# Rounded and remainder products of successive weight tiles in alternating order

## The chip, the core and the metric

One NeuronCore of a Trainium2 chip runs the kernel in one launch. TensorE (PE in the profile) multiplies, VectorE (DVE) and ScalarE (ACT) work on tiles in SBUF and PSUM, and SyncE (SP) issues the DMA transfers from HBM. The metric is the device time of one execution in microseconds (us), as the median of several runs; lower is better.

## The reference, cut

What is computed is one encoder block on 256 tokens of width 2048, all in fp32: a gated feed-forward network (half weight), a token mixing stage of 16 attention heads, and a second feed-forward network. Nine vectors that come from `silu(c) @ w_ada` shift, scale and gate the stages.

```python
def swiglu(x, w_gate, w_up, w_down):
    return (jax.nn.silu(x @ w_gate) * (x @ w_up)) @ w_down

mod = jax.nn.silu(c) @ w_ada[l] + b_ada[l]
sh1, sc1, gt1, sh2, sc2, gt2, sh3, sc3, gt3 = jnp.split(mod, N_MOD, axis=-1)
f = swiglu(modulate(rms_norm(h, g_ffn1[l]), sh1, sc1), w1_gate[l], w1_up[l], w1_down[l])
h = h + 0.5 * gt1[:, None, :] * f
...
qkv = modulate(rms_norm(h, g_mix[l]), sh2, sc2) @ w_qkv[l]
...
mix = jnp.concatenate([o_na, o_dil], axis=-1) @ w_o[l]
h = h + gt2[:, None, :] * mix
f = swiglu(modulate(rms_norm(h, g_ffn2[l]), sh3, sc3), w2_gate[l], w2_up[l], w2_down[l])
h = h + 0.5 * gt3[:, None, :] * f
```

D_MODEL is 2048, D_FF 5632, SEQ 256.

## The kernel before

**Products.** An fp32 product is made of three faster ones in the rounded type fp32r. Every weight tile of 128x1024 (eight blocks of 128x128) is brought from HBM into a buffer `raw` (tile `rw`, five buffers), rounded by ACT into `hi` (`hiw`, line 144, four buffers), and DVE writes the remainder `raw - hi` into `lo` (`low`, line 147, four buffers). The activations stand the same way in two halves side by side: `r[:, 0, :]` is rounded, `r[:, 1, :]` the remainder, 256 columns each (`nx` for the inputs of the up and gate products, `hd` for the inputs of the down products). One matmul with a block of `hi` streams both halves, 512 columns; one with a block of `lo` streams the rounded half alone, 256 columns, and adds to the first half of the same PSUM bank.

**Order on PE.** `W.add` (line 320) collects eight blocks, that is one weight tile. Then it issues the eight products with `hi` (line 338) and after them the eight with `lo` (line 340). So PE runs eight matmuls of 512 columns, eight of 256, eight of 512, and so on. A sum (one PSUM bank, or one half of a pair of banks) may begin and end inside a tile: its first `hi` product carries `start`, which clears the bank, and its last `lo` product carries `stop`. `then` is the code that reads a finished sum, such as `up_finish`, `up_fold` or the update of `h` in `ffn_down`.

**Stages.** Tiles that pass through `W.add` are numbered here from 0, in the order in which they are used, over all weight matrices:

| stage | tiles | time in the trace, us | blocks of a sum |
|---|---|---|---|
| 1a: first 6 of 16 input blocks of the up and gate products (`up_first`, tile `pa`) | 0 to 35 | 65 to 173 | 6 |
| 1b: the other 10 (`pb`) | 36 to 115 | 173 to 397 | 10 (first four pairs 6 and 4) |
| 1d: down products over 32 of 44 hidden blocks (`pd`) | 116 to 179 | 397 to 576 | 32 |
| 1c: the last 12 hidden blocks (`pb`) | 180 to 227 | 576 to 710 | 16 |
| 1e: their down products (`pd`) | 228 to 251 | 710 to 778 | 12 |
| attention: q, k, v and output projection, own order of products | 252 to 379 | 782 to 1189 | |
| 2a, 2b, 2d, 2c, 2e: the second network in the same way, no part of 6 | 380 to 643 | 1198 to 1937 | 16, 16, 32, 16, 12 |

In 1a four sums of six blocks fill three tiles: in the first tile of three both sums begin, in the second the first four blocks belong to a sum that is already open, in the third the first two do.

**What sets the order.** A scheduler orders the instructions of each engine by its own estimate of when operands are ready; inside `manual_schedule` regions the named engines follow the order of the code. Each engine then runs its queue strictly in that order. `W.prepare` (line 303) makes the cast and the remainder of a tile three tiles ahead of its use. A cast has to wait until the products with the `hi` of four tiles earlier are done, a remainder for the products with that `lo`. In the same DVE queue stand the products of `w_ada` (line 127, tiles `ra` and `rx`, 128x2048 each, paced by `ws.pace`), and in the same ACT queue the copies of finished sums in 1a (line 356, `pt<-pa`).

Of the kernel before, what the change touches and what calls it, by code (L numbers as in the profile page):

```python
# [15 lines left out]
P = 128  # L16
S = 256
D = 2048
KT = D // P
# [45 lines left out]
def build(tc, a):  # L65
    nc = tc.nc
    with ExitStack() as ctx:
# [42 lines left out]
        nx = [cp.tile([P, 2, S], F32R, tag=f"nx{k}", name=f"nx{k}") for k in range(KT)]  # L110
# [167 lines left out]
        first = {}  # L278
# [5 lines left out]
        class W:  # L284
            def __init__(self):
                self.head = 0
                self.tail = 0
                self.todo = []
                self.thens = []
                self.ready = {}  # L290
                self.rate = 0.0
                self.credit = 0.0

            def fetch(self, n):
                while self.head < n:
                    self.ready[self.head] = wraw(srcs[self.head])
                    self.head += 1
# [19 lines left out]
                self.tail += 1  # L317
                return self.ready.pop(self.tail - 1)

            def add(self, out, r, first, last, then=None, whole=False):  # L320

                self.todo.append((out, r, first, last, whole))
                if then:
                    self.thens.append(then)
                if len(self.todo) < 8:
                    return
                hi, lo = self.chunk()
                todo, thens = self.todo, self.thens  # L330
                self.todo, self.thens = [], []
                for b, (out, r, first, last, whole) in enumerate(todo):
                    w = hi[:, b * P : (b + 1) * P]
                    if whole:
                        nc.tensor.matmul(out[:, :S], w, r[:, 0, :], start=first, stop=False)
                        nc.tensor.matmul(out[:, :S], w, r[:, 1, :], start=False, stop=False)
                    else:
                        nc.tensor.matmul(out, w, r, start=first, stop=False)  # L338
                for b, (out, r, first, last, whole) in enumerate(todo):
                    nc.tensor.matmul(out[:, :S], lo[:, b * P : (b + 1) * P], r[:, 0, :], start=False, stop=last)  # L340
                for then in thens:
                    then()

# [4 lines left out]
        ws = W()  # L348
# [14 lines left out]
        def up_mm(ps, k0, k1, first, last, then=None):  # L363
            for j in range(2):
                for k in range(k0, k1):
                    end = k == k1 - 1
                    ws.add(ps[:, j, :], nx[k], first and k == k0, last and end, then if end and j else None)

        def up_finish(f, ps, part, hid):
            if f in part:  # L370
# [14 lines left out]
        def ffn_down(fs, hid, gate, stat=None, out=None, order=None):  # L385
            acc_ = {}
            for d, f in down_order(fs):
                if d not in acc_:
                    acc_[d] = bank("pd")
                if stat is not None and d == KT // 2 and f == fs[0]:  # L390
                    bg_until(0)
                if order is not None and d == KT - 4 and f == fs[0]:
                    order.enter_context(tc.manual_schedule(engines=STARTUP))
                whole = d == KT - 1 and fs[-1] == FT - 1
                end = f == fs[-1]

                def update(d=d, whole=whole):
                    ps = acc_[d]
                    if stat is not None:
                        stat.fold()  # L400
                    for part_ in (ps[:, :S], ps[:, S:])[: 1 if whole else 2]:
                        nc.vector.scalar_tensor_tensor(h[d], part_, gate(d), h[d], ALU.mult, ALU.add)  # L402
                    if stat is not None:
                        stat.add(h[d], late=d >= KT - 4)
                    if out is not None:
                        nc.sync.dma_start(out[d], h[d])

                ws.add(acc_[d], hid[f], f == fs[0], end, update if end else None, whole)

        def ffn(kx, part, ready_k, gate, stat=None, out=None, order=None):  # L410

# [64 lines left out]
        with tc.manual_schedule(engines=STARTUP):  # L476
# [53 lines left out]
        with tc.tile_pool(name="att", bufs=2) as ap_, tc.tile_pool(name="atc", bufs=1) as ac:  # L530
# [201 lines left out]
            last = [j * KT + k for k in range(K2, KT) for j in (7, 6)]  # L732
# [41 lines left out]
            last = [8 * KT + k for k in range(KT)]  # L774
# [10 lines left out]
        hid = {}  # L785
        ps2 = [pair("pb") for f in range(NG)]
        for k in range(KT):
            if k % 2 == 0 and k + 2 < KT:
                norm_pair((k + 2, k + 3), r3, 6, 7)
            for f in range(NG):  # L790
                for j in range(2):
                    ws.add(ps2[f][:, j, :], nx[k], k == 0, k == KT - 1)
        order.close()
        for f in range(NG):
            up_finish(f, ps2[f], {}, hid)
# [1 line left out]
        for f in range(NG, F1):  # L797
            ps = pair("pb")
# [108 lines left out]
```

## Time and profile before

| | us |
|---|---|
| median of 3 runs | 1945.46 |
| the runs | 1944.61, 1949.75, 1945.46 |
| the profiled execution | 1942.14 |
| its span, first to last instruction | 1940.4 |
| PE busy, share of the span | 1899.4, 98% |
| DVE busy | 1523.3, 79% |
| ACT busy | 907.5, 47% |

The profile is one execution. 1.74 us of its 1942.14 lie outside the span. PE is busy nearly all the time, but matmuls overlap in the records (the 512-column ones last about 0.39 us each and start about 0.23 us apart), so what a matmul costs is read from the distance of starts, not from its duration.

### The profile page before, as it was taken

The numbers are of one execution on the slowest core, as the hardware profiler recorded it, in microseconds if no ns is written. First come the engines' busy times: TensorE is split into PE (matmuls) and PEld (weight loads), VectorE is DVE, ScalarE is ACT, GpSimd is POOL, SyncE is SP. The second block draws the span as 40 slices with busy tenths as digits, with TensorE's granted clock in tenths as the row PEclk, the third lists the DMA queues.
The fourth block names the chain that finished last, engine by engine and source line by source line (L and its number), as shares of the span: only waits on it lengthen the run. The fifth ranks groups of instructions, "written<-read, shape, count | busy, mean of one in ns | idle before, by whom it ended". The sixth has DMA issues, their size and how long they took to land.

```text
span 1940.4 us, 27380 instructions
## 1 busy us (share of the span) xinstructions
PE 1899.4 (98%) x10504; PEld 1648.6 (85%) x10504; DVE 1523.3 (79%) x2055; ACT 907.5 (47%) x1332; POOL 0.7 (0%) x6
## 2 busy tenths in 40 slices
PE   7999999999999999899999998999999999999999
PEld 6878888888888888688888887888888888888888
DVE  7898999999878889699986898668865555555665
ACT  2444544443334454445555565544444433334442
POOL 0000000000000000000000000000000000000000
PEclk9999999999999999999999999999999999999999
DMA  9998888899989898598865544668865666666664
GB/s 392 386 340 303 315 305 309 305 329 395 356 302 345 310 321 311 171 326 324 318 222 165 163 142 146 192 213 318 323 206 186 188 190 186 190 189 187 191 194 134
DMA packets 120083, 503.98 MB, mean 260 GB/s; under 512 B 13328, under 2 KB 15632, under 8 KB 101520
## 3 DMA queue, kind: packets, MB, share of 16 engines
q1 hardware_dynamic: 119952, 502.24, 74.5%
q8 instruction: 82, 1.34, 0.3%
q14 instruction: 49, 0.40, 0.1%
HBM read 500.09 MB, written 2.10 MB: 259 GB/s over the span
## 4 chain that ended last, share of the span: by engine, by line
PE 53%; DVE 4%; issue 1%; ACT 1%; DMA 0%; SPq 0%; ACTq 0%; DVEq 0%
PE pb L338 17%; PE pb L340 9%; PE pd L338 8%; PE pd L340 4%; PE pqq L606 3%; PE pqk L606 3%; PE pqv L606 3%; DVE low L147 2%; PE pqq L609 1%; PE pqk L609 1%; PE pqv L609 1%; PE pso L643 1%; DVE wt L633 1%; PE psc L153 0%; PE po L153 0%
## 5 line engine op out<-in xcount | busy, mean ns | idle before, releaser
L144 ACT CAST hiw<-rw 128x1024 fp32r<-128x1024 f32 x644 | 675.0, 1051 | 793.8 <-PE pd L338 233.7
L147 DVE TENSOR_TENSOR low<-rw,hiw 128x1024 fp32r<-128x1024 f32 x644 | 783.4, 1221 | 293.9 <-ACT hiw L144 286.8
L338 PE MATMUL pb<-nx,hiw 128*128 128x512 f32 x2432 | 610.5, 393 | 4.1 <-DVE nx L221 4.1
L338 PEld LDWEIGHTS pb<-nx,hiw 128*128 128x128 f32 x2432 | 438.4, 189 | 83.0 <-issue 4.4
L340 PEld LDWEIGHTS pb<-nx,low 128*128 128x128 f32 x2432 | 331.7, 190 | 24.5 <-DVE low L147 0.8
L338 PE MATMUL pd<-hd,hiw 128*128 128x512 f32 x1384 | 346.7, 392 | 0.0
L340 PE MATMUL pb<-nx,low 128*128 128x256 f32 x2432 | 339.2, 282 | 0.4 <-DVE low L147 0.4
L338 PEld LDWEIGHTS pd<-hd,hiw 128*128 128x128 f32 x1384 | 248.9, 189 | 44.4
L127 DVE CUSTOM_DVE_ANT_0 ra<-ra,cb,vec 128x2048 f32<-128x2048 f32 x109 | 255.7, 2346 | 11.4 <-DMA ra<-in_w_ada_dram 11.3
L340 PEld LDWEIGHTS pd<-hd,low 128*128 128x128 f32 x1408 | 191.7, 190 | 13.6 <-DVE low L147 0.3
L340 PE MATMUL pd<-hd,low 128*128 128x256 f32 x1408 | 196.5, 282 | 0.0
L402 DVE SCALAR_TENSOR_TENSOR h<-pd,m,h 128x256 f32<-128x256 f32 x126 | 59.5, 481 | 59.4 <-PE pd L340 59.0
L127 DVE CUSTOM_DVE_ANT_0 rx<-rx,cb,vec 128x2048 f32<-128x2048 f32 x35 | 82.1, 2346 | 2.1 <-DMA rx<-in_w_ada_dram 2.1
L338 PE MATMUL pa<-nx,hiw 128*128 128x512 f32 x288 | 72.6, 394 | 6.2 <-ACT hiw L144 6.2
L606 PE MATMUL pqv<-hiw,nx 128*128 128x512 f32 x256 | 66.7, 403 | 5.4 <-ACT nx L219 5.4
L338 PEld LDWEIGHTS pa<-nx,hiw 128*128 128x128 f32 x288 | 51.7, 189 | 16.7 <-ACT hiw L144 7.4
L606 PE MATMUL pqk<-hiw,nx 128*128 128x512 f32 x256 | 65.4, 396 | 0.3 <-ACT hiw L144 0.3
L606 PE MATMUL pqq<-hiw,nx 128*128 128x512 f32 x256 | 64.6, 394 | 0.0
L643 PE MATMUL pso<-ox,hiw 128*128 128x512 f32 x248 | 64.2, 402 | 0.0
L606 PEld LDWEIGHTS pqv<-hiw,nx 128*128 128x128 f32 x256 | 48.3, 193 | 17.8 <-ACT nx L219 7.9
L606 PEld LDWEIGHTS pqk<-hiw,nx 128*128 128x128 f32 x256 | 46.4, 188 | 9.5 <-ACT hiw L144 0.7
L606 PEld LDWEIGHTS pqq<-hiw,nx 128*128 128x128 f32 x256 | 46.8, 188 | 9.1
(143 smaller groups left out, 1370.9 us busy)
## 6 DMA issues: line engine op xcount, KB each, us to landing
ra<-in_w_ada_dram SPq DMA_DIRECT2D x109, 1024.0 KB, 7.3
rw<-in_w_b_dram SPq DMA_DIRECT2D x200, 512.0 KB, 4.4
rw<-in_w_d_dram SPq DMA_DIRECT2D x128, 512.0 KB, 4.3
rw<-in_w_c_dram SPq DMA_DIRECT2D x96, 512.0 KB, 3.6
rw<-in_w_qkv_dram SPq DMA_DIRECT2D x96, 512.0 KB, 4.4
rx<-in_w_ada_dram SPq DMA_DIRECT2D x35, 1024.0 KB, 7.1
rw<-in_w_e_dram SPq DMA_DIRECT2D x48, 512.0 KB, 4.6
rw<-in_w_a_dram SPq DMA_DIRECT2D x44, 512.0 KB, 5.3
```

The source lines that it names most:

```text
L127: dot = nc.vector.tensor_tensor_reduce(out=raw, in0=raw, in1=cb, scale=1.0, scalar=vec[:, BA + i : BA + i + 1], op0=ALU.mult, op1=ALU.add, ...
L144: cast = nc.scalar.copy(hi, raw)
L147: nc.vector.tensor_tensor(lo, raw, hi.bitcast(F32), ALU.subtract)
L338: nc.tensor.matmul(out, w, r, start=first, stop=False)
L340: nc.tensor.matmul(out[:, :S], lo[:, b * P : (b + 1) * P], r[:, 0, :], start=False, stop=last)
L402: nc.vector.scalar_tensor_tensor(h[d], part_, gate(d), h[d], ALU.mult, ALU.add)
L606: nc.tensor.matmul(ps[t], nx[k][:, i, t * P : (t + 1) * P], whi[:, kk * 512 : (kk + 1) * 512], start=k + i == 0, stop=False)
L609: nc.tensor.matmul(ps[t], nx[k][:, 0, t * P : (t + 1) * P], wlo[:, kk * 512 : (kk + 1) * 512], start=False, stop=k == KT - 1)
L633: nc.vector.scalar_tensor_tensor(t, t if u < END else ps[:, :S], gt2[:, d : d + 1], rows[b], ALU.mult, ALU.mult)
L643: nc.tensor.matmul(ps, w, o, start=kk == 0, stop=False)
```

## The change

A tile now begins with remainder products where the tile before ended with them. `ended_lo` remembers this. Each block carries a `key`, the sum to which it belongs. Blocks whose sum begins in this tile can't go first with `lo`, since the `hi` product has to clear the bank over all 512 columns; they are `late`, the others are `early` if the tile before ended with `lo`. Order in a tile: `lo` of the early blocks, `hi` of all eight, `lo` of the late ones. `stop` goes to whichever product of a block comes last. A tile in which all blocks are early ends with `hi`, and the next tile begins with `hi` again.

```diff
-                self.todo.append((out, r, first, last, whole))
+                self.todo.append((out, r, first, last, whole, key))
...
+                new = {t[5] for t in todo if t[2]}
+                early = [b for b in range(8) if todo[b][5] not in new] if self.ended_lo else []
+                late = [b for b in range(8) if b not in early]
+
+                def low(b, stop):
+                    out, r = todo[b][:2]
+                    nc.tensor.matmul(out[:, :S], lo[:, b * P : (b + 1) * P], r[:, 0, :], start=False, stop=stop)
+
+                for b in early:
+                    low(b, False)
+                for b, (out, r, first, last, whole, key) in enumerate(todo):
                     w = hi[:, b * P : (b + 1) * P]
+                    stop = last and b in early
                     if whole:
                         nc.tensor.matmul(out[:, :S], w, r[:, 0, :], start=first, stop=False)
-                        nc.tensor.matmul(out[:, :S], w, r[:, 1, :], start=False, stop=False)
+                        nc.tensor.matmul(out[:, :S], w, r[:, 1, :], start=False, stop=stop)
                     else:
-                        nc.tensor.matmul(out, w, r, start=first, stop=False)
-                for b, (out, r, first, last, whole) in enumerate(todo):
-                    nc.tensor.matmul(out[:, :S], lo[:, b * P : (b + 1) * P], r[:, 0, :], start=False, stop=last)
+                        nc.tensor.matmul(out, w, r, start=first, stop=stop)
+                for b in late:
+                    low(b, todo[b][3])
+                self.ended_lo = bool(late)
```

The keys are `(id(ps), j)` in `up_mm`, `d` in `ffn_down` and `(f, j)` in stage 2a. No instruction is added or removed on any engine. The attention part, which doesn't use `W.add`, keeps its order on all engines; on DVE, ACT and SP the scheduler moves instructions of the feed-forward stages by up to five places.

How often PE goes from a `lo` to a `hi` product, counted in the built programs:

| stage | 1a | 1b | 1d | 1c | 1e | 2a | 2b | 2d | 2c | 2e |
|---|---|---|---|---|---|---|---|---|---|---|
| before | 35 | 80 | 64 | 48 | 24 | 7 | 120 | 64 | 48 | 24 |
| after | 47 | 66 | 33 | 24 | 16 | 4 | 60 | 33 | 24 | 16 |

PE in stage 1d, where tile 130 ends and tile 131 begins (`low_3858` is the remainder of tile 130, `hiw_3888` and `low_3889` are the halves of 131); before:

```order
L340 MATMUL pd_3885<-hd21_2905,low_3858 128x256
L340 MATMUL pd_3885<-hd22_2985,low_3858 128x256
L340 MATMUL pd_3885<-hd23_3038,low_3858 128x256
L338 MATMUL pd_3885<-hd24_3118,hiw_3888 128x512
L338 MATMUL pd_3885<-hd25_3175,hiw_3888 128x512
L338 MATMUL pd_3885<-hd26_3256,hiw_3888 128x512
```

and now:

```order
L340 MATMUL pd_3885<-hd21_2905,low_3858 128x256
L340 MATMUL pd_3885<-hd22_2985,low_3858 128x256
L340 MATMUL pd_3885<-hd23_3038,low_3858 128x256
L340 MATMUL pd_3885<-hd24_3118,low_3889 128x256
L340 MATMUL pd_3885<-hd25_3175,low_3889 128x256
L340 MATMUL pd_3885<-hd26_3256,low_3889 128x256
```

The eight remainder products of tile 131 have moved ahead of its eight rounded ones, so PE asks for `low_3889` when the tile begins and not eight matmuls later.

PE in stage 1a, where tile 4 ends and tile 5 begins (`low_469` belongs to tile 4, `hiw_500` and `low_501` to tile 5, a third tile of three); before:

```order
L340 MATMUL pa_550<-nx1_100,low_469 128x256
L340 MATMUL pa_550<-nx2_101,low_469 128x256
L340 MATMUL pa_550<-nx3_102,low_469 128x256
L338 MATMUL pa_550<-nx4_103,hiw_500 128x512
L338 MATMUL pa_550<-nx5_104,hiw_500 128x512
```

and now:

```order
L340 MATMUL pa_550<-nx2_101,low_469 128x256
L340 MATMUL pa_550<-nx3_102,low_469 128x256
L340 MATMUL pa_550<-nx4_103,low_501 128x256
L340 MATMUL pa_550<-nx5_104,low_501 128x256
L351 MATMUL pa_550<-nx4_103,hiw_500 128x512
```

Two remainder products of tile 5 now stand ahead of its rounded ones. In the second tile of three the scheduler also sends one to four `hi` products of the new sum ahead of the four early `lo` ones.

ACT at the same place (`pt10_573` is the copy of the sum that ends in tile 4); before:

```order
L144 CAST hiw_468<-rw_466 128x1024
L144 CAST hiw_500<-rw_498 128x1024
L356 COPY pt10_573<-pa_523 128x512
L230 ACTIVATE nx7_106<-nt_583,m0_78 128x256
L144 CAST hiw_526<-rw_524 128x1024
```

and now:

```order
L144 CAST hiw_468<-rw_466 128x1024
L370 COPY pt10_573<-pa_523 128x512
L144 CAST hiw_500<-rw_498 128x1024
L230 ACTIVATE nx7_106<-nt_583,m0_78 128x256
L144 CAST hiw_526<-rw_524 128x1024
```

The copy and the cast of tile 5 have changed places. Before, the copy of a sum that ends in tile n-1 stood directly ahead of the cast of tile n at tiles 11, 17, 26 and 32; now it does so at 5, 11, 17, 26 and 32, all of them third tiles of three.

## Rows read from the trace of the kernel before

**Rows 1.** The page's part 1, busy time of PE, PE's weight loads, DVE, ACT and POOL:

```profile
PE 1899.4 (98%) x10504; PEld 1648.6 (85%) x10504; DVE 1523.3 (79%) x2055; ACT 907.5 (47%) x1332; POOL 0.7 (0%) x6
```

**Rows 2.** Windows of 50 and 100 us in stages 1a, 1b and 2b: start:end, length, then busy us (and instructions) of PE, PEld, DVE, ACT and POOL, the granted PE clock as a share of 2.4 GHz, DMA share, GB/s:

```profile
100.00:150.00 50.00, 47.30 (x269) 40.99 (x268) 47.37 (x54) 24.29 (x32) 0.00 (x0) 1.00 0.92 342
300.00:350.00 50.00, 50.00 (x289) 44.00 (x288) 48.89 (x67) 23.98 (x33) 0.00 (x0) 1.00 0.85 292
...
1600.00:1700.00 100.00, 100.00 (x576) 88.02 (x575) 50.67 (x55) 37.76 (x36) 0.00 (x0) 1.00 0.61 188
```

**Rows 3.** Timeline of PE around one tile of stage 1d, read through slits so narrow that single matmuls show (first number: start, us): the first and the sixth `hi` product of the tile, its first `lo` product, and the first `hi` product of the next tile:

```profile
503.25 0.40 PE L338 MATMUL pd<-hd,hiw 128*128 128x512 f32 x1
...
504.41 0.39 PE L338 MATMUL pd<-hd,hiw 128*128 128x512 f32 x1
...
505.09 0.40 PE L340 MATMUL pd<-hd,low 128*128 128x256 f32 x2
...
506.04 0.40 PE L338 MATMUL pd<-hd,hiw 128*128 128x512 f32 x1
```

**Rows 4.** Timeline of PE at four places: `hi` runs of tiles 396 and 499 in stage 2b (103 tiles apart); eight 512-column products of the q, k, v projection that follow other 512-column ones, and what follows them; and the end of the kernel, where the last weight tiles run as 256-column products throughout:

```profile
1246.97 2.00 PE L338 MATMUL pb<-nx,hiw 128*128 128x512 f32 x8
...
1534.69 2.00 PE L338 MATMUL pb<-nx,hiw 128*128 128x512 f32 x8
...
871.34 1.98 PE L606 MATMUL pqv<-hiw,nx 128*128 128x512 f32 x8
873.15 1.07 PE L609 MATMUL pqv<-low,nx 128*128 128x512 f32 x4
...
1934.17 0.28 PE L335 MATMUL pd<-hd,hiw 128*128 128x256 f32 x1
...
1936.09 1.12 PE L340 MATMUL pd<-hd,low 128*128 128x256 f32 x8
```

**Rows 5.** Who waited for whom in stage 1a, 60 to 185 us (us in total, times, longest), and, as the last line, the same view of the whole span for the casts and the `hi` products of stages 1b, 1c, 2b and 2c:

```profile
ACT pt L356 <- PE pa L340: 55.4, 24, 4.2
...
PE pa L338 <- ACT hiw L144: 6.2, 5, 1.6
...
PE pa L340 <- DVE low L147: 0.6, 2, 0.4
PE pb L340 <- DVE low L147: 0.4, 1, 0.4
...
ACT hiw L144 <- PE pb L338: 171.8, 117, 2.0
```

**Rows 6.** Timeline at tile 17 of stage 1a, on PE (the `lo` run of tile 16, the `hi` run of tile 17), ACT (copy, cast) and DVE (remainder of tile 17):

```profile
114.60 1.11 PE L340 MATMUL pa<-nx,low 128*128 128x256 f32 x8
116.85 2.11 PE L338 MATMUL pa<-nx,hiw 128*128 128x512 f32 x8 [1.15 <-ACT hiw L144]
...
115.27 0.58 ACT L356 COPY pt<-pa 128x512 f32<-128x512 f32 x1 [4.25 <-PE pa L340]
115.75 1.05 ACT L144 CAST hiw<-rw 128x1024 fp32r<-128x1024 f32 x1
...
116.83 1.23 DVE L147 TENSOR_TENSOR low<-rw,hiw 128x1024 fp32r<-128x1024 f32 x1 [0.26 <-ACT hiw L144]
```

**Rows 7.** The same at tile 5: its `hi` run on PE, its cast and the copy behind it on ACT; and on PE the first `hi` run of tile 36, where stage 1b begins:

```profile
79.35 2.00 PE L338 MATMUL pa<-nx,hiw 128*128 128x512 f32 x8
...
172.85 2.00 PE L338 MATMUL pb<-nx,hiw 128*128 128x512 f32 x8
...
75.39 1.06 ACT L144 CAST hiw<-rw 128x1024 fp32r<-128x1024 f32 x1
79.07 0.59 ACT L356 COPY pt<-pa 128x512 f32<-128x512 f32 x1 [2.62 <-PE pa L340]
```

**Rows 8.** Timeline of stage 1d: on PE the `hi` run of tile 124 and both runs of tile 131; on DVE the remainders of tiles 124 and 125 and of 131 and 132, two in a row each; on ACT the cast of tile 131:

```profile
419.33 2.00 PE L338 MATMUL pd<-hd,hiw 128*128 128x512 f32 x8
...
438.89 2.00 PE L338 MATMUL pd<-hd,hiw 128*128 128x512 f32 x8
440.74 1.22 PE L340 MATMUL pd<-hd,low 128*128 128x256 f32 x8
...
419.02 2.35 DVE L147 TENSOR_TENSOR low<-rw,hiw 128x1024 fp32r<-128x1024 f32 x2
...
439.46 2.35 DVE L147 TENSOR_TENSOR low<-rw,hiw 128x1024 fp32r<-128x1024 f32 x2
...
438.50 1.06 ACT L144 CAST hiw<-rw 128x1024 fp32r<-128x1024 f32 x1 [0.53 <-DMA rw<-in_w_d_dram]
```

**Rows 9.** Idle gaps of PE and the granted clock behind them, in the attention part: timeline rows of PE (start, duration, in brackets the idle time before), then windows as in Rows 2:

```profile
1099.94 0.33 PE L663 MATMUL pT<-ident,qn 128*128 128x128 f32 x1 [2.02 <-DVE qn L589]
...
1140.23 0.39 PE L153 MATMUL po<-pl,vh 128*128 128x256 f32 x1 [1.25 <-DVE pl L157]
...
1142.59 0.80 PE L207 MATMUL pstat<-sq,ones 128*128 128x256 f32 x2 [1.07 <-ACT sq L193]
...
1100.00:1105.00 5.00, 5.00 (x28) 4.32 (x29) 5.00 (x9) 2.30 (x5) 0.00 (x0) 1.00 0.54 149
...
1143.10:1146.40 3.30, 3.30 (x9) 2.55 (x9) 2.74 (x6) 0.89 (x2) 0.00 (x0) 0.50 0.37 104
```

More of the change, by code (lines that the diff above doesn't have):

```diff
@@ L292, in __init__ @@
                 self.credit = 0.0
+                self.ended_lo = False
             def fetch(self, n):
@@ L318, in chunk, with add @@
                 return self.ready.pop(self.tail - 1)
-            def add(self, out, r, first, last, then=None, whole=False):
-                self.todo.append((out, r, first, last, whole))
+            def add(self, out, r, first, last, then=None, whole=False, key=None):
+                self.todo.append((out, r, first, last, whole, key))
                 if then:
@@ L331, in add @@
                 self.todo, self.thens = [], []
-                for b, (out, r, first, last, whole) in enumerate(todo):
+                new = {t[5] for t in todo if t[2]}
[7 more added lines that the diff above has]
+                for b, (out, r, first, last, whole, key) in enumerate(todo):
                     w = hi[:, b * P : (b + 1) * P]
+                    stop = last and b in early
                     if whole:
                         nc.tensor.matmul(out[:, :S], w, r[:, 0, :], start=first, stop=False)
-                        nc.tensor.matmul(out[:, :S], w, r[:, 1, :], start=False, stop=False)
+                        nc.tensor.matmul(out[:, :S], w, r[:, 1, :], start=False, stop=stop)
                     else:
-                        nc.tensor.matmul(out, w, r, start=first, stop=False)
-                for b, (out, r, first, last, whole) in enumerate(todo):
-                    nc.tensor.matmul(out[:, :S], lo[:, b * P : (b + 1) * P], r[:, 0, :], start=False, stop=last)
+                        nc.tensor.matmul(out, w, r, start=first, stop=stop)
+                for b in late:
+                    low(b, todo[b][3])
+                self.ended_lo = bool(late)
                 for then in thens:
@@ L366, in up_mm @@
                     end = k == k1 - 1
-                    ws.add(ps[:, j, :], nx[k], first and k == k0, last and end, then if end and j else None)
+                    ws.add(ps[:, j, :], nx[k], first and k == k0, last and end, then if end and j else None,
+                           key=(id(ps), j))
         def up_finish(f, ps, part, hid):
@@ L406, in update @@
                         nc.sync.dma_start(out[d], h[d])
-                ws.add(acc_[d], hid[f], f == fs[0], end, update if end else None, whole)
+                ws.add(acc_[d], hid[f], f == fs[0], end, update if end else None, whole, key=d)
         def ffn(kx, part, ready_k, gate, stat=None, out=None, order=None):
@@ L791, in build @@
                 for j in range(2):
-                    ws.add(ps2[f][:, j, :], nx[k], k == 0, k == KT - 1)
+                    ws.add(ps2[f][:, j, :], nx[k], k == 0, k == KT - 1, key=(f, j))
         order.close()
```

## The prediction

> **What bounds the kernel now.** First the busy times: PE is busy for 98% of the span, DVE for 79%, ACT for 47% [rows 1]. Then the same by stage, since an average hides the limits: in 2b PE is busy all the time and DVE half of it; in 1b PE again all the time, but DVE 98%; in 1a neither is full, both at 95% [rows 2]. So in the second network only PE's own pace counts, in 1b DVE is close behind, and in 1a PE, ACT and DVE wait for each other in turn. Last the pace of PE itself. Busy time doesn't show it, because records overlap, so I read starts. In a tile the first five `hi` products take 504.41 - 503.25 = 1.16 us, 0.232 each, the last three 0.68, 0.227 each; the eight `lo` products take 0.95, 0.119 each [rows 3]. Where 512-column products follow others of the same width, eight take 873.15 - 871.34 = 1.81, 0.226 each, so 0.227 is the steady pace and the first five after a `lo` run are slow. Where 256-column ones follow each other for long, sixteen take 1936.09 - 1934.17 = 1.92, 0.120 each [rows 4].
>
> **The change part by part.**
>
> Switches. A pair of switches (`lo` to `hi` and back) costs 5 x (0.232 - 0.227) = 0.026 us at the start of the `hi` run, and the eight `lo` products are 0.01 cheaper than 8 x 0.120: net 0.016. Over 103 tiles of 2b a tile takes (1534.69 - 1246.97) / 103 = 2.793 [rows 4]; without a switch it would take 8 x 0.2267 + 8 x 0.120 = 2.774, a net 0.020. I take the middle, 0.0185. The order counts in the table of the change fall from 479 to 276 outside 1a, that is by 203: 203 x 0.0185 = 3.8 us saved (3.2 to 4.1 by the two readings). It is all on PE, which sets the end in these stages. In 1a twelve switches come on top, 0.2 us, partly hidden in waits that are there anyway; I count nothing.
>
> Does the longer run keep its pace? Sixteen `lo` products in a row do, by the end of the kernel, and so do the twelve 512-column products of the projections [rows 4]. I see no row in which a run gets slower with length.
>
> A rule of the Trainium skill speaks against this term. The rows show 0.232 us for a 512-column product behind a `lo` run and 0.227 later [rows 3]. The page "TensorE: Matmul & The Clock Gate", section "Back-to-back issue gap", gives the distance of warm matmuls as the column count over 2.4 GHz plus about 2.5 ns, 216 ns for 512 columns and 109 for 256, whatever ran before. By that rule order is free and this term is 0. The trace differs from it in both numbers, and in that the predecessor matters; it is a rival below.
>
> Remainders asked for earlier, stages with room. A tile that begins with `lo` needs its remainder eight `hi` products earlier, 1.84 us (503.25 to 505.09), and releases its `hi` buffer 0.95 us later. In 1b the casts wait for PE to release a buffer, 117 times for 171.8 us in all `pb` stages [rows 5]; that is a queue that stands three tiles, over 8 us, ahead of its use. After the cast 1.05 and the remainder 1.22 there are still some 5 us of lead, minus what DVE's other work takes (a `w_ada` product is 2.35). In 2a to 2e DVE has half its time free [rows 2]. I cost both at nothing. If DVE fell behind by 4 us or more in 1b, each tile that begins with `lo` could add up to 1.84 once, not each time, since a wait of PE gives DVE the same time back.
>
> Stage 1d. Here the lead is gone at some tiles. Tile 131 begins at 438.89 and its remainder is the first of the two that start at 439.46, so it is ready at 439.46 + 1.22 = 440.68; PE used it at 440.74, just in time behind the `hi` run. Its cast had waited for its weights [rows 8]. Now tile 131 begins with `lo`: PE waits until 440.74, 1.85 us. Tile 124 begins at 419.33 and its remainder is ready at 419.02 + 1.22 = 420.24, 0.9 us late [rows 8]. The two don't add: a wait of 0.9 at 124 moves tile 131 by as much. So the sum is the largest, 1.9 us; if the weights and DVE move along with PE, both count, 2.8; if the schedulers' small moves help, 0.9.
>
> Stage 1a. Two kinds of third tiles begin with two `lo` products. At 11, 17, 26 and 32 the copy of the sum that ends in the tile before stands ahead of the cast. At tile 17 the copy runs at 115.27, the cast 115.75 to 116.80, PE starts `hi` at 116.85 after 1.15 us of idle time, and the remainder comes 116.83 to 118.06 [rows 6]. PE will now start with that remainder, 118.1 instead of 116.85: 1.2 us more, less 0.2 to 0.7 by which the copied sum now ends earlier (its four `lo` products stand first, and fewer `hi` products are ahead of its last one): 0.9. Four times that is 3.6. What is queued behind: the rest of PE's work, and by it the next copies on ACT, which wait 55.4 us for PE in this stage [rows 5]; so it isn't made good later. At tile 5 the cast ran at 75.39, long ahead of its use at 79.35 [rows 7]; now it stands behind the copy, which ends at 79.66 or some 0.6 earlier: copy, cast 1.05 and remainder 1.22 bring PE's start to 81.2 or so, 1.9 us late. Against that, PE's present waits for remainders in 1a and at tile 36, 0.6 + 0.4 = 1.0 [rows 5], go, since DVE isn't held up by PE's delay. Sum: 3.6 + 1.9 - 1.0 = 4.5 us. Bounds: DVE runs ahead while PE waits and only the last late tile counts, 1.2; nothing is made good and nothing ends earlier, 4 x 1.25 + 1.9 = 6.9.
>
> Ends of sums. A sum whose last tile ends with `hi` ends at the same time as before, since the tile holds the same products. The last sum of all likewise: nothing.
>
> Sum: -3.8 + 1.9 + 4.5 = +2.6. The profiled execution took 1942.14, so 1944.7; the median of the runs is 3.3 above it, so **1948.0 us**. The measurement of this kernel can tell about 0.3% (5.8 us) from no change; the forecast lies inside.
>
> **The rivals.**
>
> A. The delays stay hidden and the gain is whole: 1945.5 - 3.8 = 1941.7. For it: DVE has gaps in 1a, and the scheduler placed the new order by its own estimate of when remainders are ready, so it may have found room. Against: rows 6 show a chain of copy, cast and remainder with no gap in it, and the remainder wasn't on it until now.
>
> B. PE's clock falls in 1a, and the kernel is slower than before. The new waits at third tiles are gaps of 1.15 + 0.9 to 1.25, that is 2.0 to 2.4 us. A gap of 2.02 left the clock at 1.00 of 2.4 GHz; gaps of 1.25 and 1.07 us within 2.4 us of each other were followed by 3.3 us at 0.50, the 1.2 GHz level [rows 9]. The new gaps lie between. Each fall costs half of that stretch, 1.7 us. From two falls on, 1948.0 + 3.4 = 1951.4, it is slower by more than 0.3%; four give 1954.8.
>
> C. Order is free on PE, as by the rule above, and only the delays are left: 1945.5 + 1.9 + 4.5 = 1951.9. For it: some third cause might slow the products that follow each change of tile. Against: the first tile behind 512-column products has no such slow start [rows 4].
>
> D. The earlier ends of sums in 1a pull copies and casts forward, and the present waits of PE for casts, 6.2 us [rows 5], go: 1945.5 - 3.8 - 6.2 = 1935.5. Against: the third tiles now need one step more behind the cast.
>
> **How the numbers follow.** Forecast 0.50; A 0.18; B 0.20; C 0.06; D 0.06. Likeliest is the forecast, 1948.0. The range reaches down to A and, above, takes in the upper bounds of 1a and 1d (+2.4 and +0.9 on 1948.0, 1951.3), C, and three falls of B: 1941.5 to 1953.0. Left out are D and the end of B, some 0.15. Faster by over 0.3% is D alone, 0.06. Slower by over 0.3% are C and nearly all of B, 0.24. The rest, 0.70, is within 0.3%.
>
> **What the profile after would show.** In 2b two tiles take 5.57 us instead of 5.59: sixteen `hi` products 3.66 from start to start, sixteen `lo` 1.91. If they take 5.59, the first term is wrong. In 1a PE's idle time before casts becomes idle time before remainders, five waits of 2 us, and tile 36 comes about 4.5 us later than 172.85 [rows 7]; if it comes at 173 or earlier, A or D. In 1d one or two waits of PE for a remainder between 405 and 445 us that add up to 1.9. Clock 1.00 in every window from 65 to 775 us; a 0.50 there is B. It would all be wrong if DVE in 1b fell behind, which would show as PE waiting for remainders between 200 and 395 us.

## The result and the profile after

The changed kernel takes 1954.24 us (median of 5 runs, 1952.71 to 1956.58) against 1945.46 of the kernel before in the same session: ratio 1.0046, 95% interval 1.0033 to 1.006. It is slower, by 8.8 us, where 1948.0 within 1941.5 to 1953.0 was forecast. The profiled execution is the one of 1956.22. It lies 2.0 us above its median and that of the kernel before 3.3 below its own, so the two traces differ by 14 us where the medians differ by 8.8.

The busy times hide it. The page's part 1 of the changed kernel:

```profile
PE 1901.0 (97%) x10504; PEld 1652.4 (85%) x10504; DVE 1529.8 (78%) x2055; ACT 910.1 (47%) x1332; POOL 0.7 (0%) x6
```

Against [rows 1] no busy time moved by more than 7 us and PE's share fell by a point: what came in is waiting. In the new code line 351 issues the `hi` products and line 340 the `lo` products. I compare the starts of tiles. This table gives how much later a tile starts than in the kernel before (us, each in its profiled execution; the first row of numbers is the changed kernel, the others are the experiments below):

| kernel | tile 0 | 36 | 40 | 116 | 140 | 251 | 404 | 643, the last |
|---|---|---|---|---|---|---|---|---|
| the change | 0.24 | 9.94 | 11.21 | 10.92 | 15.46 | 14.41 | 16.38 | 14.07 |
| only from tile 40 on | 0.62 | 0.62 | 0.62 | 0.32 | 2.51 | 1.46 | 3.67 | 1.36 |
| filled gaps | 0.79 | 5.75 | 7.01 | 6.72 | 10.26 | 9.21 | 10.41 | 8.11 |
| 40 to 115 and from 140 on | 1.54 | 1.52 | 1.52 | 1.23 | 1.09 | 0.07 | 1.80 | -0.51 |
| fewer products in 1d | 1.15 | 9.21 | 10.48 | 10.19 | 11.90 | 18.09 | 18.66 | 16.36 |
| 116 to 139 alone | 0.56 | 0.54 | 0.55 | 0.55 | 4.89 | 4.86 | 6.56 | 6.56 |
| the same, paced | 0.19 | 0.20 | 0.20 | 0.20 | 3.15 | 3.26 | 5.89 | 5.89 |
| the same, no loads | 1.31 | 1.29 | 1.29 | 1.29 | 3.65 | 3.63 | 5.64 | 5.64 |
| without the third tiles | 1.60 | 8.10 | 7.70 | 7.41 | 7.27 | 6.26 | 9.14 | 6.84 |

Tile 0 is reached at slightly different times in every execution. From 251 to 404 lies the attention part, whose order is the same in all these kernels; it was shortest in the profiled execution of the kernel before, so every row gains lateness there. The other steps between columns are what counts. The change loses 10.97 us up to tile 40 and 4.54 from 116 to 140. In the other stages it gains.

**Stage 1a.** Who waited for whom, 60 to 195 us, PE's own waits in the changed kernel (us in total, times, longest):

```profile
PE pa L340 <- DVE low L147: 10.1, 5, 2.2
PE pb L340 <- DVE low L147: 1.6, 1, 1.6
PE pa L351 <- ACT hiw L144: 1.6, 1, 1.6
```

In [rows 5] it was 6.2 us in five waits for casts. One of the five, 1.6, is the start of tile 0 and stays (third line). The other four, 4.6 us, have become 11.7 us in six waits for remainders. The timeline at tile 17, PE, ACT and DVE (compare [rows 6]):

```profile
118.92 0.63 PE L340 MATMUL pa<-nx,low 128*128 128x256 f32 x4
121.78 0.50 PE L340 MATMUL pa<-nx,low 128*128 128x256 f32 x2 [2.23 <-DVE low L147]
...
118.89 0.59 ACT L370 COPY pt<-pa 128x512 f32<-128x512 f32 x1 [3.40 <-PE pa L351]
119.37 1.05 ACT L144 CAST hiw<-rw 128x1024 fp32r<-128x1024 f32 x1
...
117.63 2.35 DVE L127 CUSTOM_DVE_ANT_0 ra<-ra,cb,vec 128x2048 f32<-128x2048 f32 x1
119.90 0.68 DVE L371 TENSOR_TENSOR pt<-pt,pa 128x512 f32<-128x512 f32 x1
120.50 1.22 DVE L147 TENSOR_TENSOR low<-rw,hiw 128x1024 fp32r<-128x1024 f32 x1
```

It is the forecast chain: copy 118.89, cast 119.37 to 120.42, remainder 120.50 to 121.72, PE at 121.78 after 2.23 us of idle time, where [rows 6] have 1.15.

**The clock.** Windows around the gaps at tiles 11, 17 and 32 (columns as in [rows 2]: the number behind POOL is the granted clock):

```profile
98.00:102.20 4.20, 2.02 (x13) 1.60 (x12) 4.10 (x7) 2.48 (x3) 0.00 (x0) 1.00 0.79 311
102.20:105.60 3.40, 3.40 (x13) 2.91 (x12) 2.63 (x3) 0.25 (x1) 0.00 (x0) 0.50 1.01 393
118.00:122.70 4.70, 2.47 (x14) 2.01 (x13) 4.70 (x6) 2.87 (x4) 0.00 (x0) 1.00 0.94 336
122.70:126.10 3.40, 3.40 (x12) 2.81 (x11) 2.83 (x3) 0.00 (x0) 0.00 (x0) 0.50 0.88 269
166.00:170.50 4.50, 2.32 (x14) 1.88 (x13) 4.41 (x7) 2.47 (x3) 0.00 (x0) 1.00 0.97 394
170.50:173.90 3.40, 3.40 (x10) 2.70 (x9) 3.37 (x3) 0.00 (x0) 0.00 (x0) 0.50 0.89 318
```

Behind gaps of 2.18, 2.23 and 2.18 us PE runs 3.4 us at 0.50, the 1.2 GHz level, three times. The next tiles (12, 18 and 33) start late by 1.32, 1.56 and 1.57 us more. The gaps at tiles 5, 26 and 38 (1.72, 1.79, 1.63) left the clock at 1.00. By an estimate, 3.4 us at half the clock cost at most 1.7. In the kernel before 65 to 195 us has no such stretch.

**Stage 1b and the second network.** PE at the start of tile 36, at tile 38, and three starts of `hi` runs in stage 2b:

```profile
182.79 2.00 PE L351 MATMUL pb<-nx,hiw 128*128 128x512 f32 x8
...
190.22 0.50 PE L340 MATMUL pb<-nx,low 128*128 128x256 f32 x2 [1.63 <-DVE low L147]
...
1531.56 3.82 PE L351 MATMUL pb<-nx,hiw 128*128 128x512 f32 x16
1535.22 2.08 PE L340 MATMUL pb<-nx,low 128*128 128x256 f32 x16
1537.13 3.82 PE L351 MATMUL pb<-nx,hiw 128*128 128x512 f32 x16
```

Tile 36 starts at 182.79 instead of 172.85 [rows 7]. Tile 38 is a third tile of the same kind as those of 1a, and I had left it out. In 2b two tiles take 1537.13 - 1531.56 = 5.57, as forecast: 3.66 for sixteen `hi`, 1.91 for sixteen `lo`.

**Stage 1d.** PE (waits at tiles 128 and 131), DVE (a `w_ada` product, remainders, updates of `h`) and SP's queue, 427 to 453 us:

```profile
444.75 2.36 PE L340 MATMUL pd<-hd,low 128*128 128x256 f32 x16 [0.33 <-DVE low L147]
452.97 1.22 PE L340 MATMUL pd<-hd,low 128*128 128x256 f32 x8 [1.26 <-DVE low L147]
...
441.20 2.35 DVE L127 CUSTOM_DVE_ANT_0 ra<-ra,cb,vec 128x2048 f32<-128x2048 f32 x1 [4.19 <-DMA ra<-in_w_ada_dram]
443.47 2.36 DVE L147 TENSOR_TENSOR low<-rw,hiw 128x1024 fp32r<-128x1024 f32 x2
447.86 2.34 DVE L127 CUSTOM_DVE_ANT_0 rx<-rx,cb,vec 128x2048 f32<-128x2048 f32 x1
450.13 1.65 DVE L417 SCALAR_TENSOR_TENSOR h<-pd,m,h 128x256 f32<-128x256 f32 x4
451.70 2.35 DVE L147 TENSOR_TENSOR low<-rw,hiw 128x1024 fp32r<-128x1024 f32 x2
...
427.68 4.94 SPq L138 DMA_DIRECT2D rw<-in_w_d_dram  x3
432.67 0.42 SPq L121 DMA_DIRECT2D ra<-in_w_ada_dram  x1
```

What SP's weight loads waited for, 398 to 470 us (us in total, times, longest; more rows between the second and the last):

```profile
SPq L138 <- DVE low L147: 38.1, 16, 6.8
SPq L138 <- DVE m L134: 9.7, 8, 2.7
...
SPq L138 <- ACT hiw L144: 0.6, 2, 0.3
```

DVE stands still for 4.19 us at a `w_ada` product whose load SP issued at 432.67, 8.53 us before the product started, behind three weight loads that took it 4.94 us to issue. Those wait for buffers that come free when DVE has made a remainder. Two remainders, of tiles 128 and 129, stand behind the product; PE gets them late, and those of 131 and 132 late again.

### The profile page after: what moved, and what is told of

It is laid out like the page before. It is cut to its first block, busy times and chain, and to the rows that moved or that the text cites. A ratio compares the mean times of both kernels' runs of the same rounds, so it can differ in the third digit from the quotient of the medians.

```text
span 1954.4 us, 27393 instructions
## 1 busy us (share of the span) xinstructions
PE 1901.0 (97%) x10504; PEld 1652.4 (85%) x10504; DVE 1529.8 (78%) x2055; ACT 910.1 (47%) x1332; POOL 0.7 (0%) x6
## 4 chain that ended last, share of the span: by engine, by line
PE 52%; DVE 4%; issue 1%; ACT 1%; DMA 0%; SPq 0%; ACTq 0%; DVEq 0%
PE pb L351 17%; PE pb L340 9%; PE pd L351 8%; PE pd L340 4%; PE pqq L621 3%; PE pqv L621 3%; PE pqk L621 2%; DVE low L147 2%; PE pqq L624 1%; PE pqv L624 1%; PE pqk L624 1%; PE pso L658 1%; PE psc L153 1%; DVE wt L648 0%; PE pso L663 0%
## 5 line engine op out<-in xcount | busy, mean ns | idle before, releaser
L351 PE MATMUL pb<-nx,hiw 128*128 128x512 f32 x2432 | 587.3, 392 | 4.1 <-DVE nx L221 4.1
L351 PEld LDWEIGHTS pb<-nx,hiw 128*128 128x128 f32 x2432 | 446.3, 189 | 90.0 <-issue 4.8
L351 PE MATMUL pd<-hd,hiw 128*128 128x512 f32 x1384 | 332.6, 391 | 0.0
L340 PEld LDWEIGHTS pb<-nx,low 128*128 128x128 f32 x2432 | 315.5, 191 | 15.9 <-DVE low L147 2.0
L340 PE MATMUL pb<-nx,low 128*128 128x256 f32 x2432 | 320.0, 283 | 1.6 <-DVE low L147 1.6
L340 PEld LDWEIGHTS pd<-hd,low 128*128 128x128 f32 x1408 | 181.9, 191 | 12.2 <-DVE low L147 4.6
L340 PE MATMUL pd<-hd,low 128*128 128x256 f32 x1408 | 185.5, 283 | 3.4 <-DVE low L147 3.4
L390 ACT COPY gu<-pb 128x512 f32<-128x512 f32 x56 | 32.9, 587 | 145.0 <-PE pb L351 145.0
L391 DVE TENSOR_TENSOR gu<-gu,pb 128x512 f32<-128x512 f32 x56 | 38.5, 687 | 78.2 <-ACT gu L390 77.9
L351 PE MATMUL pa<-nx,hiw 128*128 128x512 f32 x288 | 77.9, 408 | 1.6 <-ACT hiw L144 1.6
```

Source lines behind the costliest of these rows:

```text
L351: nc.tensor.matmul(out, w, r, start=first, stop=stop)
L390: nc.scalar.copy(t, ps[:, :, :S])
L391: nc.vector.tensor_tensor(t, t, ps[:, :, S:], ALU.add)
```

## The experiments

All gates are on the number n of the tile in `W.add`; `early` is the list of blocks whose `lo` products come first. The kernel before took 1945.01, 1945.15, 1945.21 and 1945.63 us in the four sessions.

**1. No early remainders in 1a.**

```diff
-                early = [... if todo[b][5] not in new] if self.ended_lo else []
+                n = self.tail - 13
+                early = [... if todo[b][5] not in new] if self.ended_lo and n >= 40 else []
```

> The change, but no tile before tile 40 begins with its remainder products (stage 1a and the start of 1b are as before). Theory: of the 8.8 us lost in the medians, stage 1a holds the waits for remainders (four of about 1.2 us, 2.0 at tile 5, 1.8 at tile 38) and the clock falls that follow them; without them the trace stands at tile 40 where the kernel before stood (184.7 us, within 0.3), no clock fall between 65 and 190 us, and only stage 1d's delay (4.5) against the saved switches (3.8) is left: 1946 us (1945 to 1948). Rival: the loss is spread, by the order of DVE and ACT in later stages and the attention part; then 1950 or more.

Measured: 1943.5 us, ratio 0.9996 [0.9987, 1.0005], below what was expected. The loss up to tile 40 is gone to the last hundredth, so is the clock at 0.50 there; 1d still loses something, but 2.2 and not 4.5. What early remainders ahead of tile 40 cost, with all that hangs on them, is 1954.24 - 1943.5 = 10.7 us; the trace of the change gives 10.97 up to tile 40.

**2. Only where there is room.** As 1, with `(40 <= n < 116 or n >= 140)`.

> As the run above, and tiles 116 to 139 (the first part of stage 1d) as before too. Theory: 1d's 4.5 us were waits for remainders that were asked for before they were ready, so they go, and the saved switches are left alone: 0.020 us for each of some 185, 3.6 us, so 1941.8 us (1941 to 1943), and tile 136 begins within 0.5 us of 453.0. Rival: the 1d delay comes from DMA and DVE falling behind in 1b, where PE now runs faster; then 1d keeps 2 us or more of it and the time is 1945 or more.

Measured: 1941.02 us, ratio 0.9979 [0.997, 0.9988]: faster than both kernels. 1d loses nothing. This splits the change in three: before to this version -4.0 (switches), this to version 1 +2.5 (1d), version 1 to the change +10.7 (1a and 38). That the parts add up to +9.2 is no proof, since they are differences along one chain of kernels; by their intervals each is known to some 2 us, and the last one crosses two sessions.

**3. Filled gaps.** The change, with eight products with a block of zeros (made at the start, not shown) ahead of the six late remainders.

```diff
+                if self.tail - 13 in (5, 11, 17, 26, 32, 38):
+                    for _ in range(8):
+                        out, r = todo[early[0]][:2]
+                        nc.tensor.matmul(out[:, :S], zero, r[:, 0, :], start=False, stop=False)
```

> The change as it is, with eight additional matmuls of 256 columns ahead of the two early remainder products at tiles 5, 11, 17, 26, 32 and 38; their weights are zeros, so they add nothing to the sums. They fill about 1.0 us of each gap of 2.2. Theory: the clock falls in 1a come from these gaps; with the gaps down to 1.2 the granted clock stays at 1.00 from 65 to 190 us and the tiles still wait for their remainders: tile 40 begins some 4.5 us earlier than in the change's trace, 191.4 instead of 195.9, and the time is 1950 us (1949 to 1951.5). Rival: the falls have another cause (they come in this stage with a chance of their own, or the kernel's start sets them); then falls are seen again and the time is 1954, or 1955 to 1960 if the additional matmuls delay tiles that had no wait.

Measured: 1950.26 us, ratio 1.0032 [1.0019, 1.0044]. Windows 65 to 195 us, first this kernel, then (next fence) the change:

```profile
65.00:195.00 130.00, 122.97 (x708) 106.87 (x709) 116.20 (x132) 60.93 (x80) 0.00 (x0) 1.00 0.86 317
```

```profile
65.00:195.00 130.00, 117.75 (x633) 100.98 (x634) 115.04 (x131) 58.55 (x77) 0.00 (x0) 0.96 0.82 305
```

PE is kept at work, the remainders are as late as before, and the clock stays at 1.00. Tile 40 comes 6.2 us late instead of 11.0. So 4.7 of the 11.0 is the clock, 6.2 is the waits. The timed runs agree in size (4.0 us between the medians, and no run of the one reaches the other's), though the intervals of the ratios overlap. Three gaps of 1.23 to 1.26 us were left in this execution, at 11, 17 and 32, and none was followed by half clock.

**4. All but the third tiles.** As 1, with `n not in (5, 11, 17, 26, 32, 38) and not 116 <= n < 140`.

> The change in all tiles but 5, 11, 17, 26, 32, 38 and 116 to 139. Nothing is left out. Theory (the six tiles are the whole loss of 1a, and its other tiles lose 1.9 us of old waits for remainders): 1.9 us less than the version with the change in tiles 40 to 115 and from 140 on (1941.0), so 1939. Rival (what the other tiles gave back came only from the delays at those six, as remainders had time to run ahead): 1941.0, no gain. Second rival (a new wait at a tile that begins with remainders behind one of the six): above 1941.

Measured: 1947.17 us, ratio 1.0009 [0.9999, 1.002]: the second rival. The waits move into the second tiles of three, ahead of their four early `lo` products, at 7, 13, 19, 28 and 34, so that tiles 8, 14, 20, 29 and 35 start late (0.9 and four times 1.36 more). PE and DVE at tile 13:

```profile
109.32 0.73 PE L341 MATMUL pa<-nx,low 128*128 128x256 f32 x4 [1.08 <-DVE low L147]
...
105.77 2.35 DVE L127 CUSTOM_DVE_ANT_0 rx<-rx,cb,vec 128x2048 f32<-128x2048 f32 x1
108.04 1.22 DVE L147 TENSOR_TENSOR low<-rw,hiw 128x1024 fp32r<-128x1024 f32 x1
```

These tiles haven't the time to spare for their remainders either: here a `w_ada` product is ahead of it on DVE. In the changed kernel they were on time, it seems because the wait at the third tile before had let DVE run ahead. Gaps of 1.1 us left the clock at 1.00.

**5. Stage 1d alone.** `116 <= n < 140`.

> The change in tiles 116 to 139 alone; all other tiles as before. Nothing is left out. By the forecast's step for 1d 1.9 us is lost between tiles 116 and 140, less 12 pairs of switches, 0.2: 1945.0 + 1.7 = 1946.7. By the 4.5 us that the changed kernel lost there: 1949.3, if the loss doesn't depend on the state in which the stage begins; if it does (2.2 in the kernel that has the change from tile 40 on), about 1947. In the trace the waits of PE for a remainder stand at tiles 120, 124, 131 and 135, and their sum tells which.

Measured: 1948.65 us, ratio 1.0016 [1.0007, 1.0025]; the trace loses 4.3 between tiles 116 and 140 (0.58 at 120, 0.32 at 124, 0.34 at 129, 1.40 at 131, 1.46 at 135). So the loss is larger than the forecast's 1.9 also when nothing came before it, but it isn't a constant: 2.2, 3.5, 4.3 and 4.5 in four kernels that do the same in these tiles.

**6. Fewer `w_ada` products in 1d.** The change with `RBD = 0.25` instead of 0.45.

> The changed kernel with RBD 0.25 instead of 0.45: of 64 tiles of 1d 16 instead of 29 bring a w_ada product with them, and 13 move into 1c and 1e. Nothing is left out. Theory (1d loses its 4.5 us because remainders stand on DVE behind w_ada products that wait for their loads): the waits of PE for remainders between tiles 116 and 140 go, tile 140 stands within 0.5 us of where it stands against before at tile 116 (+10.9), and the run is 3.5 to 4.5 us shorter than that of the change, 1950 by its median of 1954.2, unless DVE's products in 1e come too late for PE. Rival (the loss comes from hi buffers that a tile which begins with its remainders gives back 0.95 us later, so that casts come late whatever DVE does): the same steps of +0.6, +0.4, +2.2, +1.4 remain and the time stays at 1954.

Measured: 1958.7 us, ratio 1.0074 [1.0056, 1.0091], which neither theory expected. Tiles 116 to 140 lose 1.7 instead of 4.5, but DVE runs twelve products there as in the change; from tile 131 on they stand one or two remainders later in its queue. That speaks for the order on DVE, but the number of products there isn't what changed. The products put off are wanted in 1e, where tiles 228 to 251 lose 5.4, most of it in one wait of 3.55 us at tile 243 with half clock behind it. The total says nothing of 1d.

**7. Stage 1d alone, paced.**

```diff
-                    self.credit += self.rate
+                    m = self.head - 13
+                    self.credit += self.rate * (0.2 if 116 <= m < 136 else 1.4 if 136 <= m < 180 else 1.0)
...
```

> The change in tiles 116 to 139 alone (as the run that took 1948.65), and of the w_ada products of 1d some 7 moved from tiles 116 to 135 into tiles 136 to 179, where DVE has time again; the number in 1d stays about the same, none is forced into 1e. Nothing is left out. Theory (remainders stand on DVE behind w_ada products, and these wait for loads that SP issues behind weight loads which wait for their buffers): the waits of PE at tiles 124, 131 and 135 go, what is left at 120 is 0.6 us or less, tile 140 stands within 0.8 us of where it stood against before at tile 116, and the run takes 1945 to 1946. Rival (the loss comes from the hi buffers that are given back later, or from the beginning of the stage itself): 4 us are lost again and the run takes 1948 to 1949.

Measured: 1947.46 us, ratio 1.001 [1.0, 1.002]; 2.95 lost. It missed: up to 440 us DVE ran the same products at the same places (421.78, 430.35 and 437.02, against 421.90, 430.51 and 437.18 in experiment 5). Only the wait at tile 135 went. From 440 to 470 us DVE ran four products here as there, but the remainders that PE asks for at 135 now stood ahead of the product that waits for its load, and not behind it:

```profile
448.74 2.35 DVE L147 TENSOR_TENSOR low<-rw,hiw 128x1024 fp32r<-128x1024 f32 x2
452.00 2.35 DVE L127 CUSTOM_DVE_ANT_0 ra<-ra,cb,vec 128x2048 f32<-128x2048 f32 x1 [0.91 <-DMA ra<-in_w_ada_dram]
```

**8. Stage 1d alone, `w_ada` products without loads.**

```diff
-            nc.sync.dma_start(raw, a["w_ada"][i])
+            if 111 <= at_tile[0] < 130:
+                unread.add(i)
+            else:
+                nc.sync.dma_start(raw, a["w_ada"][i])
...
-                out=raw, in0=raw, in1=cb, ...
+                out=raw, in0=cb if i in unread else raw, in1=cb, ...
...
```

> The change in tiles 116 to 139 alone (4.3 us lost between tiles 116 and 140 in its trace), and the 11 w_ada products that are asked for at tiles 111 to 129 read a vector that is on the chip already: their loads of w_ada are left out, the products stay on DVE in their place and length. The output isn't the reference's for that. Theory L (what is lost at tiles 128 to 135 comes from loads that SP issues behind weight loads and on which DVE stands, with remainders queued behind): the waits at 120 and 124 stay, 0.9 us, those at 128 to 135 go, 3.4 us: 1948.65 - 3.4, about 1945.3. Theory P (it is the products' own time on DVE): most of the waits stay, 1947.5 to 1948.7. Rival (hi buffers given back later): 4.3 us as before, 1948.7.

Measured: 1947.39 us, ratio 1.001 [1.0001, 1.002]; 2.4 lost. There were seven such products, not eleven, from 406 to 430 us. DVE's last two without a load, then the first with a long wait, and PE at tile 137:

```profile
426.13 2.34 DVE L132 CUSTOM_DVE_ANT_0 ra<-cb,vec 128x2048 f32<-128x2048 f32 x1
429.61 2.34 DVE L132 CUSTOM_DVE_ANT_0 rx<-cb,vec 128x2048 f32<-128x2048 f32 x1
...
455.79 2.35 DVE L132 CUSTOM_DVE_ANT_0 ra<-ra,cb,vec 128x2048 f32<-128x2048 f32 x1 [3.45 <-DMA ra<-in_w_ada_dram]
458.07 2.36 DVE L152 TENSOR_TENSOR low<-rw,hiw 128x1024 fp32r<-128x1024 f32 x2
...
459.34 1.21 PE L346 MATMUL pd<-hd,low 128*128 128x256 f32 x8 [1.14 <-DVE low L152]
```

The time lies 2 us above what theory L expected and just under what P did, since fewer loads were left out than planned and tile 137 came late anew. In the trace theory L holds in place: the waits at 120 and 124 stay (0.58, 0.32), where products stand close on DVE; those at 129, 131 and 135 (3.2 in experiment 5) are gone. And where a product waits 3.45 us for its load again, the tile behind its remainders, 137, loses 1.28. The `hi` buffers are given back as late as before (from 398 to 470 us casts wait 30.6 us for PE, 24.5 in experiment 5), so that rival is out as the cause of these waits. So the loads cause them. Whether it is their place behind the weight loads isn't separated from a second reading: without them the DMA engines were busy for 0.64 of the time from 400 to 440 us, where experiment 5 has 0.90, so a load may also take long because the engines are full.

**9. The same, products left out.** A copy of one column instead of the product and its load.

> As the run before it, but the products themselves are left out too (12 of them; a copy of one column stands in their place), with their loads. The output isn't the reference's for that. Theories L and P alike: no wait of PE for a remainder between tiles 116 and 140, tile 140 as far behind the kernel before as tile 116 was (within 0.3 us), 1944.5 to 1945. Rival (hi buffers, or the beginning of the stage): 4.3 us are lost all the same, 1948.7.

Measured: 1947.3 us, ratio 1.0013 [1.0004, 1.0023]; 2.0 lost. It didn't do what it should: the next products of the list moved up, and DVE ran as many in 400 to 440 us as in experiment 5. It decides nothing.

**10 to 12. The price of a change of width on PE.** The second network alone: `hi` and `lo` product by block in the kernel before (10), the same on version 2 (11), and runs of four in the kernel before (12).

```diff
                         nc.tensor.matmul(out, w, r, start=first, stop=False)
+                    if self.tail - 13 >= 380:
+                        nc.tensor.matmul(out[:, :S], lo[:, b * P : (b + 1) * P], r[:, 0, :], start=False, stop=last)
...
```

> The kernel before, but in the second network (stages 2a to 2e, 264 tiles) the remainder product of each block stands directly behind its rounded product: runs of one. Theory, a price for each change of width (0.0185 us for a pair of switches): eight pairs for each tile in place of one, 7 x 0.0185 x 264 = 34 us slower, 1980 us. Rival, no price for the change, only a state that builds up in a run: the first rounded product behind a remainder product took 0.233 and the first remainder product 0.113, together 0.346, under 0.2267 + 0.120; then a tile takes 2.77 instead of 2.793, 6.6 us faster, 1939 us.

> The version with the change only in tiles 40 to 115 and 140 to 251 (1941.0), and in the second network remainder behind rounded product block by block instead of in runs of eight. Nothing is left out. If a tile of the second network takes 2.773 us in every execution, as in the profiled run with blocks, against 2.783 of the change: 1941.0 - 264 x 0.010 = 1938.4. Rival (the block order has a second, longer time in most executions, as its run with 1937 to 1941 and 1951 to 1955 had): a median near 1951, with some executions near 1938.

> The kernel before, with runs of four instead of eight in the second network (four rounded products, their four remainder products, and again). Nothing is left out. If each pair of switches costs the 0.020 us that the change saves for each pair that it takes away: two pairs in a tile, 2.793 + 0.020 = 2.813 us, 264 x 0.020 = 5.3 us more, 1950.3. Rival (the price hangs on the place within a run: the first four rounded products behind remainders take 0.233, 0.236, 0.228 and 0.232, the first remainder 0.113 and the others 0.120 as in the rows): 2 x (0.929 + 0.473) = 2.804, 2.9 us more, 1947.9. Third (only long runs of remainders cost, as the block order without any price says): below 2.793.

Measured: (10) 1952.31 us, ratio 1.0021 [0.9999, 1.0044], ten runs in two groups, three from 1937.5 to 1941.4 and seven from 1951.3 to 1955.2. (11) 1952.4, ratio 1.0027 [1.001, 1.0043], two runs at 1938.8 and 1939.8 and ten from 1950.4 to 1955.0. (12) 1947.43, ratio 1.0017 [1.0007, 1.0027]. PE at two tiles of the second network that lie 168 tiles apart, in (10), then (11), then (12):

```profile
1337.15 0.39 PE L338 MATMUL pb<-nx,hiw 128*128 128x512 f32 x1
...
1803.07 0.39 PE L338 MATMUL pb<-nx,hiw 128*128 128x512 f32 x1
```

```profile
1338.67 0.40 PE L352 MATMUL pb<-nx,hiw 128*128 128x512 f32 x1
...
1813.55 0.40 PE L352 MATMUL pb<-nx,hiw 128*128 128x512 f32 x1
```

```profile
1336.35 0.40 PE L338 MATMUL pb<-nx,hiw 128*128 128x512 f32 x1
...
1807.87 0.40 PE L338 MATMUL pb<-nx,hiw 128*128 128x512 f32 x1
```

The profiled execution of (10) is of the shorter group, that of (11) of the longer one, with the same order of products: 465.92 / 168 = 2.773 us a tile against 474.88 / 168 = 2.827. In (12) it is 471.52 / 168 = 2.807, near the 2.804 that the place in the run gave (2.793 in [rows 4], 2.783 in the change). So a width change has no fixed price; what a product costs hangs on the rhythm around it.

## Why the prediction was wrong

**Switches, -3.8: right.** Version 2 has 194 fewer pairs of switches than the kernel before and is 4.0 us faster, 0.021 a pair. From tile 404 to the last the change has 114 fewer and gains 16.38 - 14.07 = 2.31 us, 0.020 a pair. In the table all kernels with the new order there gain 2.30 to 2.31, and those with the old order (116 to 139 alone) 0.00. The price belongs to this pair of orders; experiments 10 to 12 show that it isn't one of every change of width.

**Rival C, order is free: wrong.** Runs of eight, sixteen and four take 2.793, 2.783 and 2.807 us a tile, the same in every stretch of an execution. The rule of the Trainium skill ("TensorE: Matmul & The Clock Gate", section "Back-to-back issue gap") has only the column count in it, and the section gives it for a single isolated product. Here the order counts, as the forecast had it.

**Stage 1a, +4.5: the step that failed.** It measured 10.7 by the timed runs and 10.97 in the trace. Its chain was right: five waits of about 2 us behind copy, cast and remainder, tile 5's cast now behind the copy. Tile 5 lost 2.0 (1.9 forecast), tiles 11, 17, 26 and 32 lost 1.1, 1.1, 0.8 and 1.1 (0.9 each), the old waits gave back 1.9 (1.0 forecast). Two things were left out. One is tile 38, just behind the stage, 1.84 with the same chain: I cut 1a at tile 36 and took all of 1b as a stage with lead. The other is the clock: three falls to half clock, put at nothing in the forecast's sum: 4.4 us by the late tiles and 4.7 by the filled gaps. That was rival B, with the right place and nearly the right price (1.7 each forecast, 1.5 found). I gave it 0.20, because one gap of 2.02 in [rows 9] had left the clock at 1.00. A single gap that passed was no reason to put five new ones of 2.0 to 2.4 on the safe side; the same gap was followed by half clock in three of the fourteen profiled executions, as the last section shows.

**Stage 1d, +1.9: mis-sized.** It took 2.5 by the timed runs and 4.5 in the profiled execution. The sentence that failed is "The two don't add: a wait of 0.9 at 124 moves tile 131 by as much." It does move the tile, but DVE doesn't gain that time: its `w_ada` products wait for loads, and these stand in SP's queue behind weight loads that wait for buffers which DVE's own remainders give back. That the loads hold DVE is shown by experiment 8; the rest of the ring is read from the trace, and how much of the wait is the queue and how much the full DMA engines stays open. So every late remainder costs anew. I also didn't list all of them: tile 120, whose remainder came 0.5 us after the tile's start in the kernel before, and 128 and 135.

**Remainders in 1b and the second network, nothing: right.** No wait of PE for a remainder from tile 40 to 115 or from 140 on.

**Rivals A and D: wrong.** No delay of 1a stayed hidden. D's price was also misread: of the 6.2 us in [rows 5] 1.6 is the start of tile 0, which no order of later tiles could give back.

**The sum.** -4.0 + 2.5 + 10.7 = +9.2, where -3.8 + 1.9 + 4.5 = +2.6 was forecast. The parts reach past the measured +8.8 by 0.4, since they come from two sessions. In the trace of the change the same parts are 10.97, 4.54 and -3.65, together 11.9; that is one execution, 2.0 us above its median, and what the others lost less isn't known. The upper bound, 1953.0, counted three falls or the bounds of 1a and 1d, but not falls on top of the larger waits.

## What to carry to other kernels

An order of products that is cheaper in itself is worth only as much as the slack of the operands that it wants earlier: read that slack tile by tile, the tiles just behind a stage's border too, and apply the order only where it is there (here -4.0 us instead of +8.8). Late remainders cost anew each time when the engine that makes them is itself held by loads; "the largest counts" needs proof. And a new gap on PE has two prices, the gap and the half clock behind it: where the trace shows one outcome for a gap of that size, the other one still belongs in the sum.

## What was not expected of the hardware

- Products with 512 and 256 columns in turn have two steady rhythms, 0.230 + 0.117 and 0.236 + 0.117 us from start to start, and an execution keeps one of them through the second network: some 14 us apart over its 264 tiles (0.054 a tile). What chooses it stays open.
- Of six gaps of 2.18 to 2.23 us, three in the change and three at the same tiles in experiment 6, five were followed by 3.4 us at 0.50 of 2.4 GHz and one of 2.18 wasn't, nor were those of 1.6 to 1.8, six in the same two kernels. The gap of 2.02 in [rows 9] stands in all fourteen profiled executions, 2.01 to 2.02 us long, and was followed by half clock in three (experiments 4, 5 and 11); the pair of 1.25 and 1.07 was in four, the kernel before among them. In experiment 5, with the windows as in [rows 2]:

```profile
1105.19 0.33 PE L679 MATMUL pT<-ident,qn 128*128 128x128 f32 x1 [2.01 <-DVE qn L605]
...
1106.30:1109.60 3.30, 3.30 (x13) 2.91 (x12) 3.30 (x7) 1.16 (x2) 0.00 (x0) 0.50 0.61 154
```

So the length of the gap doesn't decide alone, and what does stays open. The Trainium skill ("TensorE: Matmul & The Clock Gate", section "HAM oscillation — how this bites in real kernels") describes a kernel in which every wait for data, about 3 to 5 us there, is followed by work at half clock; here the waits were shorter, and only some of them were.
